# Value products over ranked experts, gathered by rank, with a register branch for each tile

## The chip, the cores and the metric

The kernel runs on one NeuronCore of one Trainium2 chip. The metric is the device time of one execution in microseconds, taken as the median over several runs of the same program. Profiles and traces are of one profiled execution each.

## The reference, cut to what matters

The program is two transformer blocks on 256 tokens of width 2048. Block 1 is a state-space mixer and a sparse attention; block 2 is a pair of linear-attention mixers followed by an expert layer (PEER) and a final normalisation. Only the expert layer is touched by the change:

```
xn: 256 tokens x 2048
s1, s2 = scores of 128 keys each, for 8 heads          # from xn @ w_query and the sub-keys
v1, i1 = top_k(s1, 16);  v2, i2 = top_k(s2, 16)
best, pos = top_k(v1[:, None] + v2[None, :], 16)        # 16 experts for each head and token
expert = i1[pos // 16] * 128 + i2[pos % 16]             # one of 16384
gate = softmax(best)
hid = gelu(xn . u_tab[expert])
y[token] = sum over heads and k of gate * hid * v_tab[expert]
out = rmsnorm(h + y) * g
```

A token uses 8 x 16 = 128 of the 16384 experts, so 128 tokens (one token tile) make 16384 choices, many of them of the same expert. `u_tab` and `v_tab` are 16384 x 2048 in float32, 128 MiB each.

## The kernel before

All large products are made from float32 operands in two float32r parts (high and low), three matmuls for one product. Weights come as blocks of [128, 1024] float32 (512 KB) through a `Stream` (class at line 43): SyncE loads a block into `raw` (line 138), ScalarE makes the high part `wh` (line 150), VectorE the low part `wl` (line 151); three buffers of each, refilled in the order of use. The stream's order is written down in `run` (line 1712): the weights of block 1, of block 2, then `pu` (the u table, 256 blocks) and `pv` (the v table, 256 blocks).

Instructions keep the order in which the program text issues them on each engine. Work that is to lie beside the matmuls is a Python generator in `self.bg`; `step()` (line 1031) issues its next piece, `behind()` (line 1036) the same but not ahead of the latest weight split and matmul. `mm_b` calls such a hook after each half tile of matmuls.

The expert layer (`peer`, line 1529) has these stages:

- Queries (`pqy`): 16 tiles, with the scores and the top-16 searches of the first token tile behind them.
- U stage (`u_phase`, line 1595): all 16384 experts, as 128 tiles of 128 experts, for all 256 tokens: `pu` [128 experts, 256 tokens] is 16 k-tiles x 3 = 48 matmuls of 128x128x256, then a gelu on ScalarE into `WA` (tiles 0 to 63) or `WB` (64 to 127) in SBUF. Behind the first 64 tiles lies the `routing` generator (line 1437: one piece a tile), which ends in `RT`: for each token its 128 slots' key numbers n1, n2 and the gate in three bfloat16 parts.
- Gates (`gates`, line 1495): for 4 tokens at a time VectorE builds one-hot matrices `gA` (key n2, line 1507) and `gB` (key n1, 64 values, times the three gate parts, lines 1508 and 1511); 12 matmuls of 64 columns (`pg`, line 1524) sum the gate of each expert, and VectorE multiplies them into `WA` (line 1526). For `WA` this lies behind the second half of the U stage, for `WB` behind the first half of the value stage.
- Value stage (lines 1619 to 1678): all 128 tiles of experts, in two halves x two column halves x 64 blocks. A block of V [128 experts, 1024 columns] is multiplied with the activations of its experts (`h`, split in two at lines 174 and 175): 2 token tiles x 2 column chunks x 3 = 12 matmuls of 128x128x512 into four PSUM accumulators (line 1655), so 24 for each tile of experts.
- The end (lines 1680 to 1697): the last three blocks are multiplied one token tile after the other, so that the first token tile is normalised and written while the second is still multiplied.

Every tile of experts is multiplied with both token tiles, whether or not a token is routed to one of its experts; the gate is then zero. The functions that the diff touches:

## Time and profile before

| what | value |
|---|---|
| median of three runs | 3203.23 us (3198.74 to 3209.94) |
| profiled execution, its own time | 3198.8 us |
| its span, first to last instruction | 3198.8 us |
| PE busy | 3098.4 us, 97% |
| DVE busy | 2201.7 us, 69% |
| ACT busy | 1447.2 us, 45% |
| POOL busy | 242.9 us, 8% |
| DMA | 531.90 MB, mean 166 GB/s |

PE is the TensorE matmul row, PEld its weight loads, DVE is VectorE, ACT ScalarE, POOL GpSimd, SP SyncE. Matmuls are pipelined, so the time of one in a row is longer than the pace at which they follow each other; the pace is read from their start times. A group of rows gives count, busy time and mean duration, then the idle time of the engine before them and who ended it.

### The profile page before, as it was taken

The page shows a single profiled execution, that of the slowest core. Times are in us where ns is not written, and L with a number is a line of the kernel's source. Part 1 is how long each engine was busy: PE and PEld are TensorE (multiplying, and loading weights), DVE is VectorE, ACT ScalarE, POOL GpSimd, SP SyncE. Part 2 cuts the span into 40 slices and gives each one's busy share as a digit, 9 for nine tenths or more (in the row PEclk, how much of TensorE's full clock was granted, in tenths as well). Part 3 has the DMA queues.
Part 4 walks back from the last instruction along what each step waited for, and adds up shares of the span by engine and source line. Part 5 has one row for each costly group of instructions (what it writes and reads, how often), then busy time and mean ns, then how long its engine had stood idle before and what let it go on. Part 6 is the DMA issues. An engine that isn't in the chain of part 4 may idle for free.

```text
span 3198.8 us, 52021 instructions
## 1 busy us (share of the span) xinstructions
PE 3098.4 (97%) x21016; PEld 2793.0 (87%) x21016; DVE 2201.7 (69%) x3382; ACT 1447.2 (45%) x2034; POOL 242.9 (8%) x171
## 2 busy tenths in 40 slices
PE   7988999999997999899999999999999999999998
PEld 7987899888786999788899999999998777788787
DVE  8857544555666763575586776588886999965655
ACT  4464333544445573354434444433334444444544
POOL 4453000000001000210001001000000000000000
PEclk8889999999998999999999999999999999999999
DMA  4134645434464543226655555555556555555554
GB/s 167 66 138 160 217 165 173 142 140 145 165 225 145 191 140 117 81 100 210 198 167 178 185 180 183 178 168 170 169 168 212 175 174 170 173 186 189 185 189 167
DMA packets 144465, 531.90 MB, mean 166 GB/s; under 512 B 16736, under 2 KB 17760, under 8 KB 141920
## 3 DMA queue, kind: packets, MB, share of 16 engines
q1 hardware_dynamic: 143648, 526.49, 49.2%
q8 instruction: 164, 2.69, 0.3%
q10 hardware_dynamic: 576, 2.10, 0.2%
q14 instruction: 77, 0.63, 0.1%
HBM read 522.23 MB, written 6.29 MB: 165 GB/s over the span
## 4 chain that ended last, share of the span: by engine, by line
PE 84%; issue 6%; DVE 6%; POOL 2%; ACT 2%; DMA 0%; POOLq 0%; DVEq 0%; ACTq 0%
PE pu L210 22%; PE acc L1655 22%; PE pz L225 9%; PE pq L210 4%; PE pso L225 4%; PE pqy L210 3%; PE pcv L210 3%; PE pk L210 2%; DVE wl L151 2%; PE pg L1524 1%; PE pi L225 1%; PE pv L225 1%; PE pf L210 1%; PE pz L1300 1%; PE pq L1289 1%
## 5 line engine op out<-in xcount | busy, mean ns | idle before, releaser
L151 DVE TENSOR_TENSOR wl<-raw,wh 128x1024 fp32r<-128x1024 f32 x940 | 1195.2, 1273 | 686.2 <-ACT wh L150 683.8
L150 ACT ACTIVATE wh<-raw 128x1024 fp32r<-128x1024 f32 x943 | 995.3, 1056 | 1130.3 <-PE pu L210 378.3
L210 PE MATMUL pu<-h,wh 128*128 128x256 f32 x4096 | 745.3, 283 | 1.3 <-ACT qy L1580 1.3
L1655 PE MATMUL acc<-wh,h 128*128 128x512 f32 x2040 | 659.2, 399 | 1.3 <-DVE h L175 0.7
L210 PEld LDWEIGHTS pu<-h,wh 128*128 128x128 f32 x4096 | 630.1, 188 | 1.5 <-ACT qy L1580 1.5
L210 PE MATMUL pu<-h,wl 128*128 128x256 f32 x2048 | 577.2, 282 | 1.4 <-DVE wl L151 1.4
L1655 PEld LDWEIGHTS acc<-wh,h 128*128 128x128 f32 x2040 | 384.4, 188 | 93.3 <-DVE h L175 1.1
L1655 PE MATMUL acc<-wl,h 128*128 128x512 f32 x1020 | 404.3, 396 | 0.0
L210 PEld LDWEIGHTS pu<-h,wl 128*128 128x128 f32 x2048 | 386.3, 189 | 2.2 <-DVE wl L151 2.2
L225 PE MATMUL pz<-wh,t 128*128 128x512 f32 x1024 | 335.9, 400 | 0.0
L1655 PEld LDWEIGHTS acc<-wl,h 128*128 128x128 f32 x1020 | 192.2, 188 | 43.9 <-DVE wl L151 0.3
L225 PEld LDWEIGHTS pz<-wh,t 128*128 128x128 f32 x1024 | 192.5, 188 | 40.6 <-issue 1.0
L225 PE MATMUL pz<-wl,t 128*128 128x512 f32 x512 | 201.4, 393 | 1.6 <-DVE wl L151 1.4
L225 PE MATMUL pso<-wh,t 128*128 128x512 f32 x640 | 200.6, 393 | 0.3 <-DVE th L984 0.3
L1511 DVE TENSOR_TENSOR gB<-gB,rt 128x256 bf16<-128x256 bf16 x384 | 151.1, 421 | 5.5
L174 ACT ACTIVATE h<-WA 128x256 fp32r<-128x256 f32 x127 | 52.8, 418 | 207.3 <-PE acc L1655 207.3
L225 PEld LDWEIGHTS pso<-wh,t 128*128 128x128 f32 x640 | 120.2, 188 | 27.1 <-DVE th L984 0.7
L210 PE MATMUL pq<-t,wh 128*128 128x256 f32 x768 | 138.1, 283 | 0.0
L174 ACT ACTIVATE h<-WB 128x256 fp32r<-128x256 f32 x128 | 53.6, 419 | 182.4 <-PE acc L1655 182.4
L225 PE MATMUL pso<-wl,t 128*128 128x512 f32 x320 | 124.8, 390 | 0.3 <-DVE wl L151 0.3
L210 PEld LDWEIGHTS pq<-t,wh 128*128 128x128 f32 x768 | 117.1, 188 | 0.7 <-issue 0.3
L225 PEld LDWEIGHTS pz<-wl,t 128*128 128x128 f32 x512 | 96.5, 188 | 22.6 <-DVE wl L151 2.3
(555 smaller groups left out, 4456.2 us busy)
## 6 DMA issues: line engine op xcount, KB each, us to landing
raw<-pu SPq DMA_DIRECT2D x256, 512.0 KB, 3.6
raw<-pv SPq DMA_DIRECT2D x256, 512.0 KB, 3.8
raw<-w_z SPq DMA_DIRECT2D x96, 512.0 KB, 3.2
raw<-w_fqi SPq DMA_DIRECT2D x48, 512.0 KB, 3.3
raw<-w_a_in SPq DMA_DIRECT2D x32, 512.0 KB, 3.3
raw<-w_q SPq DMA_DIRECT2D x32, 512.0 KB, 3.2
raw<-w_b_out SPq DMA_DIRECT2D x32, 512.0 KB, 4.0
raw<-w_conv SPq DMA_DIRECT2D x32, 512.0 KB, 3.2
```

The lines of the kernel that those rows point to most:

```text
L150: self.nc.scalar.activation(h, t, AF.Copy)
L151: m = (engine or self.nc.vector).tensor_tensor(l, t, h.bitcast(F32), op=OP.subtract).ins
L174: self.nc.scalar.activation(h, x, AF.Copy)
L210: mm = nc.tensor.matmul(ps, a[:, c], b(k), start=(k == 0 and n == 0), stop=(k == nk - 1 and n == len(ops) - 1))
L225: self.nc.tensor.matmul(pss[tt], x[a](k)[:, ts], b[:, kk * 512:(kk + 1) * 512], start=(k == 0 and n == 0), stop=(k == nk - 1 and n == 2))
L1289: pe.matmul(p4[:, g_], f8(N[c])[:, g_, :], half(Y8)[:, g_], start=True, stop=True)
L1300: pe.matmul(pz[:, g_, :], f8(Xs[c])[:, g_, :], Q8[:, g_, :], start=True, stop=True)
L1511: v.tensor_tensor(B[:, n], B[:, 0], bc(RT[2 + n][:, ts], 64), op=OP.mult)
L1524: pe.matmul(ps[:, j, :], A[:, j], B[:, n, j], start=(n == 0), stop=(n == 2))
L1655: pe.matmul(acc[t][e], x[:, t * 128:(t + 1) * 128], y[:, e * 512:(e + 1) * 512], start=(n == 0 and q == 0), stop=(n == 63 and q == len(ops ...
```

## The change

What it does, in the order of the program:

- `routing` is hooked twice for each U tile (as `behind` in `mm_b`) and so lies behind the first 32 tiles instead of 64. `RT` is one tile instead of five.
- The gelu of a U tile goes to a small buffer and from there by a DMA on ScalarE's queue to a DRAM tile `WG` [16384 experts, 512]: the first 256 columns of a row are the expert's activations for the 256 tokens.
- `gates` runs once, over all 128 values of n1, behind U tiles 32 and up, three pieces a tile. The one-hot matrices have the 4 tokens innermost. A further matmul a token (`cnt`) counts, for each expert and token tile, how often it is chosen. ScalarE copies the gates to a staging tile, and for each 64 tokens eight DMAs on ScalarE's queue write them to the second 256 columns of the rows of `WG`, in runs of 64 x 4 = 256 bytes. The product of gate and activation is no longer made here.
- `sort` (new) follows `gates`: it ranks the experts in four classes (chosen by both token tiles, by the first only, by the second only, by none), makes the list `idx` of expert numbers by rank, and four tile counts `cuts`, read into registers at U tile 123.
- The stream no longer holds `pv`. For each tile of 128 ranks GpSimd gathers the rows of V (8 KB each, [128, 2048]) and the rows of `WG` (2 KB each) by an indirect DMA; GpSimd multiplies gate and activation, ScalarE and VectorE split both operands.
- The value products of a tile lie in two `If` blocks on PE, one for each token tile (12 matmuls each: 4 column chunks x 3), the gathers and the split in `If` blocks of their engines. The ranks are taken in the order 0, 54, 1, 55, ..., 53, 107, 108, ..., 127. All eight accumulators [128, 512] are kept to the end, opened by eight matmuls of zeros.
- The end: both token tiles are added, normalised and written after the last product.

```diff
 # gates
+        nt, ng = 4, 64
...
+            A = P.tile([128, 128, nt], BF16, name="gA", bufs=2)
+            E = P.tile([128, 128, nt], BF16, name="gE", bufs=2)
+            B = P.tile([128, 3, 128, nt], BF16, name="gB", bufs=2)
+            bc = lambda n: RT[:, n, None, ts].to_broadcast([128, 128, nt])
+            v.tensor_tensor(A, self.iota4, bc(1), op=OP.is_equal)
+            v.tensor_tensor(E, self.iota4, bc(0), op=OP.is_equal)
+            v.tensor_tensor(B, E[:, None, :, :].to_broadcast([128, 3, 128, nt]),
+                            RT[:, 2:5, None, ts].to_broadcast([128, 3, 128, nt]), op=OP.mult)
...
+            A, E, B = AB.pop(b)
+            if b * nt % ng == 0:
+                st = self.stage.tile([128, 128, ng], F32, name="gst", bufs=2)
+            ps = self.psum.tile([128, nt, 128], F32, tag="g", name="pg", bufs=2)
...
+                    pe.matmul(ps[:, j, :], A[:, :, j], B[:, n, :, j], start=(n == 0), stop=(n == 2))
+                pe.matmul(cnt[:, half, :], A[:, :, j], E[:, :, j], start=(first and j == 0), stop=(last and j == nt - 1))
+            o = b * nt % ng
+            act.activation(st[:, :, o:o + nt], ps.rearrange("p t n -> p n t"), AF.Copy)
+            if o + nt == ng:
+                for n in range(0, 128, 16):
+                    t0 = b * nt + nt - ng
+                    nc.scalar.dma_start(G[n * 128:(n + 16) * 128, t0:t0 + ng].rearrange("(n p) t -> p n t", p=128),
+                                        st[:, n:n + 16, :])
 # sort (its core: 32 batches of 4 keys)
+            for o, a in ((A, 0), (E, 1)):
+                v.tensor_tensor(o, self.iota4, pb[:, a, None, ts].to_broadcast([128, 128, nt]), op=OP.is_equal)
+            v.tensor_tensor(B[:, 0:2], E[:, None, :, :].to_broadcast([128, 2, 128, nt]),
+                            self.nv[:, :, None, ts].to_broadcast([128, 2, 128, nt]), op=OP.mult)
...
+                pe.matmul(L, A[:, :, j], B[:, 0:2, :, j], start=(b + j == 0), stop=(b == nb - 1 and j == nt - 1))
 # peer
+        NR, NS, NV = 32, 78, 54
...
+        order = [j for n in range(NV) for j in (n, n + NV)] + list(range(2 * NV, 128))
...
+                raw[q] = vr.tile([128, D], F32, name="vraw", bufs=4)
+                with tc.If(reg["load"] > j):
+                    gp.indirect_dma_start(out=raw[q], out_offset=None, in_=i["pv"],
+                                          in_offset=bass.IndirectOffsetOnAxis(ap=idx[:, j:j + 1], axis=0))
...
+                wg[q] = vr.tile([128, 2, T], F32, name="wg", bufs=4)
+                with tc.If(reg["load"] > j):
+                    gp.indirect_dma_start(out=wg[q].rearrange("p a t -> p (a t)"), out_offset=None, in_=WG[:, :],
+                                          in_offset=bass.IndirectOffsetOnAxis(ap=idx[:, j:j + 1], axis=0))
...
+        for n in range(128):
+            ps = self.psum.tile([128, T], F32, tag="u", name="pu", bufs=2)
+            self.mm_b(ps, X, hook=(self.behind if n < NR else self.step) if n else None)
...
+            if n >= NR:
+                self.step()
+            w = rp.tile([128, T], F32, name="w", bufs=4)
+            act.activation(w, ps, AF.Gelu)
+            nc.scalar.dma_start(WG[n * 128:(n + 1) * 128, 0:T], w)
...
+                self.bg = chain(self.gates(rp, RT, WG[:, T:2 * T], cnt), self.sort(rp, cnt, idx, cuts))
+            elif n == 123:
+                self.finish()
+                regs()
+                for q in range(4):
+                    gather_v(q)
...
+            wh, wl = [vs.tile([128, D], F32R, name=n, bufs=3) for n in ("vwh", "vwl")]
...
+            with tc.If(reg["split"] > j):
+                gp.tensor_tensor(hm, g[:, 0], g[:, 1], op=OP.mult)
+                act.activation(hh, hm, AF.Copy)
+                v.tensor_tensor(hlo, hm, hh.bitcast(F32), op=OP.subtract)
+                act.activation(wh, r, AF.Copy)
+                v.tensor_tensor(wl, r, wh.bitcast(F32), op=OP.subtract)
...
+        def mm(q, t):
+            wh, wl, hh, hlo = hl[q]
+            ts = slice(t * 128, (t + 1) * 128)
+            for e in range(4):
+                es = slice(e * 512, (e + 1) * 512)
+                for a, b in ((hh, wh), (hh, wl), (hlo, wh)):
+                    pe.matmul(acc[t][e], a[:, ts], b[:, es], start=False, stop=True, skip_group_check=True)
+
+        prep(0)
+        for q in range(128):
+            j = order[q]
+            gather_v(q + 4)
+            gather_w(q + 3)
+            prep(q + 1)
+            with tc.If(reg["first"] > j):
+                mm(q, 0)
+            with tc.If(reg["end"] > j):
+                with tc.If((reg["both"] > j) | (reg["second"] <= j)):
+                    mm(q, 1)
...
+        for t in range(2):
+            for e in range(4):
...
+                v.tensor_tensor(o, o, acc[t][e], op=OP.add)
+                act.activation(acc[t][e], o, AF.Square, accum_out=sq[:, t, e:e + 1])
```

## Rows read from the trace of the kernel before

**Rows 1.** The page: busy time of each engine, and granted TensorE clock by slice.
```profile
PE 3098.4 (97%) x21016; PEld 2793.0 (87%) x21016; DVE 2201.7 (69%) x3382; ACT 1447.2 (45%) x2034; POOL 242.9 (8%) x171
PEclk8889999999998999999999999999999999999999
```

**Rows 2.** Busy time by stretch: U stage (four stretches), value stage (two), end, queries.
```profile
core 0: us, PE busy (x) PEld busy (x) DVE busy (x) ACT busy (x) POOL busy (x), PEclk, DMA share, GB/s
1670.70:1738.00 67.30, 66.99 (x559) 66.79 (x558) 45.51 (x66) 27.71 (x35) 5.22 (x2) 1.00 0.55 174
1738.00:2051.00 313.00, 311.91 (x2596) 311.28 (x2595) 206.34 (x346) 134.98 (x168) 18.84 (x11) 1.00 0.58 182
2051.50:2402.00 350.50, 350.50 (x3460) 347.42 (x3459) 306.21 (x491) 134.53 (x169) 0.00 (x0) 1.00 0.54 169
2439.00:2790.00 351.00, 349.78 (x2131) 273.90 (x2130) 337.29 (x606) 156.57 (x231) 0.00 (x0) 1.00 0.53 181
2790.00:3190.00 400.00, 399.88 (x1715) 320.69 (x1711) 241.33 (x294) 196.12 (x292) 6.86 (x5) 1.00 0.55 182
1580.00:1670.00 90.00, 88.83 (x745) 88.63 (x743) 74.17 (x205) 34.72 (x45) 4.22 (x7) 1.00 0.57 179
```

**Rows 3.** PE in order of time, at the seam of U and value stage (start, us).
```profile
2438.72 0.29 PE L210 MATMUL pu<-h,wl 128*128 128x256 f32 x1
2438.84 0.40 PE L210 MATMUL pu<-h,wh 128*128 128x256 f32 x2
2439.08 0.28 PE L210 MATMUL pu<-h,wl 128*128 128x256 f32 x1
2439.20 3.60 PE L1655 MATMUL acc<-raw,WA 128*128 128x512 f32 x8
2442.63 0.86 PE L1524 MATMUL pg<-gB,gA 128*128 128x64 bf16 x24
```

**Rows 4.** Groups of instructions by line, U stage with routing (1672 to 2050).
```profile
L151 DVE TENSOR_TENSOR wl<-raw,wh 128x1024 fp32r<-128x1024 f32 x130 | 175.9, 1358 | 122.4 <-ACT wh L150 120.9
```

**Rows 5.** The same, U stage with gates (2051.5 to 2402).
```profile
L151 DVE TENSOR_TENSOR wl<-raw,wh 128x1024 fp32r<-128x1024 f32 x112 | 136.4, 1218 | 0.0
L150 ACT ACTIVATE wh<-raw 128x1024 fp32r<-128x1024 f32 x113 | 119.8, 1060 | 217.5 <-PE pu L210 164.2 <-DVE gB L1508 51.3 <-DVE wl L151 2.0
L1511 DVE TENSOR_TENSOR gB<-gB,rt 128x256 bf16<-128x256 bf16 x189 | 74.6, 422 | 4.1
L1507 DVE TENSOR_TENSOR gA<-iota,rt 128x512 bf16<-128x512 bf16 x63 | 43.0, 682 | 0.0
```

**Rows 6.** The same, second half of the value stage (2800 to 3180).
```profile
L175 DVE TENSOR_TENSOR h<-WB,h 128x256 fp32r<-128x256 f32 x128 | 56.1, 438 | 78.5 <-ACT h L174 78.5
L174 ACT ACTIVATE h<-WB 128x256 fp32r<-128x256 f32 x128 | 53.6, 419 | 182.4 <-PE acc L1655 182.4
```

**Rows 7.** Single lines: count, duration in ns min/median/max, first and last start.
```profile
L1605 ACT ACTIVATE WB<-pu x64: 363/366/370, 2049.6 to 2441.1; 128x256 f32<-128x256 f32 x64
L1432 POOL TENSOR_TENSOR cand<-val x16: 619/624/627, 1595.0 to 1909.6; 128x256 f32<-128x256 f32 x16
L138 SPq DMA_DIRECT2D raw<-pv x256: 327/328/885, 2427.2 to 3175.7; - x128
```

**Rows 8.** ScalarE's DMA issues in order of time: start, us, count.
```profile
0.73 2.33 ACTq L297 DMA_DIRECT2D t<-xT  x4
```

**Rows 9.** DMA queues (packets, MB, share of 16 engines) and issues (KB, us to landing).
```profile
q8 instruction: 164, 2.69, 0.3%
raw<-pv SPq DMA_DIRECT2D x256, 512.0 KB, 3.8
ident<-ident SPq DMA_DIRECT2D x2, 64.0 KB, 3.7
```

**Rows 10.** The end in order of time: start, us, instruction.
```profile
3189.68 1.28 DVE L1645 TENSOR_TENSOR h<-h,acc 128x512 f32<-128x512 f32 x2
3189.77 0.39 PE L1655 MATMUL acc<-wh,h 128*128 128x512 f32 x1
3192.77 1.28 DVE L1687 SCALAR_TENSOR_TENSOR h<-h,ssf,h 128x1024 f32<-128x1024 f32 x1 [0.67 <-POOL ssf L604]
3194.32 0.43 SPq L1688 DMA_DIRECT2D out<-h  x1
```

**Rows 11.** A stretch in which PE waits, columns as in the stretches above.
```profile
960.00:1040.00 80.00, 62.33 (x394) 54.76 (x393) 55.72 (x86) 43.18 (x69) 15.03 (x13) 0.89 0.41 144
```

More of the change, by code (lines that the diff above doesn't have):

```diff
@@ L17 @@
 AX = mybir.AxisListType
+ET = mybir.EngineType
 PSUM = bass.MemoryType.PSUM
@@ L1608, in peer @@
[L1608 to L1619 removed]
+        rt = lambda shape, name, dt=F32: rp.tile([128] + shape, dt, name=name)
@@ new lines, in peer, with regs @@
+        gp.memset(self.ones, 1.0)
+        gp.memset(self.smask, 1.0)
+        gp.memset(self.smask[:, :, 0:1], 0.0)
+        mhalf = rt([2], "mhalf2")
+        gp.memset(mhalf, -0.5)
+        RT = self.RT = rt([5, T], "rt", BF16)
+        idx = rt([128], "idx", U32)
+        cuts = rt([4], "cuts", I32)
+        WG = self.dram.tile([16384, 2 * T], F32, name="WG")
+        left, stage = ExitStack(), ExitStack()
+        NR, NS, NV = 32, 78, 54
+        reg = {}
+        def regs():
+            for k, n, engines in (("both", 0, (ET.PE,)), ("first", 1, (ET.PE,)), ("second", 2, (ET.PE,)),
+                                  ("end", 3, (ET.PE,)), ("load", 3, (ET.Pool,)),
+                                  ("split", 3, (ET.Activation, ET.DVE, ET.Pool))):
+                reg[k] = nc.values_load(cuts[0:1, n:n + 1], engines=engines, min_val=0, max_val=128)
@@ L1625, in peer @@
         sq = self.small.tile([128, 2, 4], F32, name="sqf")
-        order = [(half, c, n) for half in range(2) for c in range(2) for n in range(64)]
-        parts = {}
-        def part(m):
-            if m < len(order):
-                half, c, n = order[m]
-                if m == 0:
-                    parts[m] = W[half][:, n, :]
-                    return
-                r = ring[:, m % 4]
-                self.split(r[:, 0], r[:, 1], W[half][:, n, :])
-                parts[m] = r
-        self.bg = self.gates(rp, W[1], RT, 64)
@@ L1658, in peer @@
-        te = [(t, e) for t in range(2) for e in range(2)]
-        late = []
-        for m, (half, c, n) in enumerate(order):
-            if n == 0:
-                acc = [[self.psum.tile([128, 512], F32, tag="acc", name="acc", bufs=4) for _ in range(2)] for _ in range(2)]
-            if m + 2 == 128:
-                self.finish()
-            part(m + 2)
-            w, r = s.get(), parts.pop(m)
-            if m + 3 >= len(order):
-                late.append((n, w, r))
-                continue
-            for t, e in te:
-                mm(n, w, r, t, e)
-            if not half:
-                self.step(1 + (n % 8 == 0))
-            if n == 63:
-                for t, e in te:
-                    done(half, c, t, e)
@@ L1678, in peer @@
-        ss = self.small.tile([128, 2], F32, name="ssf")
-        def write(t):
+        stage.close()
+        vs = right.enter_context(tc.tile_pool(name="vs", bufs=1, side="right"))
+        pes.close()
+        self.psum = pes.enter_context(tc.tile_pool(name="psum3", bufs=1, space=PSUM))
+        acc = [[self.psum.tile([128, 512], F32, name=f"acc{t}{e}") for e in range(4)] for t in range(2)]
+        z = vs.tile([128, 512], BF16, name="zero")
+        gp.memset(z, 0.0)
+        for q in range(3):
+            gather_w(q)
@@ L1681, in write @@
+        ss = self.small.tile([128, 2], F32, name="ssf")
+        for t in range(2):
+            for e in range(4):
+                cs = slice(e * 512, (e + 1) * 512)
+                o = hs[t][:, cs]
+                v.tensor_tensor(o, o, acc[t][e], op=OP.add)
+                act.activation(acc[t][e], o, AF.Square, accum_out=sq[:, t, e:e + 1])
+                if e < 2:
+                    gp.tensor_tensor(o, o, fg[:, cs], op=OP.mult)
             r = ss[:, t:t + 1]
@@ L1727, in run @@
             s.add(i[n])
-        pv = i["pv"].rearrange("(n p) d -> n p d", p=128)
-        for half in range(2):
-            for c in range(2):
-                pvc = pv[64 * half:64 * half + 64, :, c * 1024:(c + 1) * 1024]
-                if half + c == 0:
-                    s.add(pvc[0:1], split=False)
-                    pvc = pvc[1:]
-                s.add(pvc)
         g1 = ExitStack()
```

187 lines of the change are left out of this document (116 added, 71 removed).

## The prediction

> **What bounds the kernel now.** I read the page first: PE is busy 97% of the span and its granted clock is full from the first third on [rows 1]. Then the stretches [rows 2]: in the U stage and in the value stage PE is busy for all but some 2 us in 1430, while DVE ranges from 60 to 96% and the DMA engines from 53 to 58%. So in both stages the number of matmuls times their pace is the time, and no wait has to be looked for. The paces are start-to-start times: 0.12 us for a 128x128x256 product of the U stage [rows 3], 400/1715 = 0.233 us for a 128x128x512 product [rows 2], 0.86/24 = 0.036 us for a gate product of 64 columns [rows 3]. The U stage runs from 1670.7 to 2439.2 us [rows 2, 3], 768.5 us; its 128 x 48 products make 737 of them, 768 gate products 28. The value stage runs to 3190.2 (last product, [rows 10]), 751 us, and 8.6 us of normalising and writing follow to 3198.8.
>
> **How many products are left.** This is a count of the data, not a time. I followed the reference's routing on its given inputs: 6376 experts are chosen by both token tiles, 3694 by the first only, 3757 by the second only, 2557 by none. The class borders lie at 6376, 10070 and 13827, so the tile counts are 50, 79 (first), 78 (start of the second) and 109. The first token tile needs 79 tiles, the second 50 + 31 = 81: 160 of 256 half tiles, 1920 products instead of 3072. Nineteen tiles of 128 are empty.
>
> **Value stage.** 1920 x 0.233 = 448 us on PE instead of 751: **-303**. What comes next behind PE, for each of 109 tiles, against PE's 448/109 = 4.1 us:
> - DMA: 1 MB of V and 0.25 MB of WG, 1.31 million bytes. A stretch with 182 GB/s at a share of 0.55 gives 331 GB/s for a full share [rows 2], so 4.0 us. This is the next limit, 4% away.
> - DVE: a low part of twice the size, 2 x 1.22, and one activation split 0.44 [rows 5, 6]: 2.9 us. ACT: 2 x 1.06 + 0.42 = 2.5 us [rows 5, 6].
> - GpSimd: 0.62 for the product [rows 7] and the issue of two gathers. No DMA issue by GpSimd is in the trace. From below, SP holds 0.33 us for one [rows 7]; ScalarE 2.33/4 = 0.58 [rows 8]; from above, an issue that holds GpSimd until it lands costs 3.8 [rows 9]. I take 0.58, the nearest issue row: 1.8 us a tile; the range is 1.3 to 8.2.
> - Branches: no row shows one. PE has 12 products, 2.8 us, ahead of a jump if the operands are there, so I take the 58 jumps over one arm in the 109 tiles as hidden; from above a jump waits for code as for a DMA, up to 3.7 us [rows 9].
>
> The order pairs 24-product tiles with 12-product tiles and four buffers of V smooth the rest, but with DMA at 96% of PE's time I add 5%: **+22**.
>
> **U stage.** Gates: 768 products of now 128 columns and 256 counts, 1024 in all. Their price lies between 0.036 (if the weight load sets the pace) and 0.072 (if the columns do); half the 256-column pace is 0.06, and I take it: 61 us. The sort adds 128 products of 256 columns at 0.12: 15 us. Of the 28 us of gates that stood here nothing remains, and 4 us of scores and seams stay: 737 + 61 + 15 + 4 = 817 against 768.5, **+49** (from +24 to +61). What lies beside these products:
> - Routing now has 32 tiles x 5.76 = 184 us. DVE needs 64 x 1.36 = 87 for low parts [rows 4]; its other work in the first 380 us was 45.5 + 206.3 - 175.9 = 76 [rows 2, 4], some 4 of it gates. That is 159 of 184 us, 86%. The queries had the same density of pieces: DVE 74.2 of 90 us, PE 88.8 [rows 2]. 1.3% of 184: **+3**.
> - Gates: a tile now has 1.5 batches of 16 products, 5.76 + 1.44 = 7.2 us on PE. DVE: 512 elements in 0.68 and 256 in 0.42 [rows 5], so 1536 in 1.72 at the same slope; 2 x 1.22 + 1.5 x (0.68 + 0.68 + 1.72) = 7.1 us. It is near the limit even if the new layout brings nothing; before, DVE ran at 337 of 351 us with PE losing 1.2 [rows 2]. **+3**.
> - ScalarE: 2 x 1.06, the gelu 0.37 [rows 7], the new PSUM copy of 512 columns at most twice that, 0.73 x 1.5, one DMA issue for WG 0.58 and 8 in 10.7 tiles for the gates 0.43: 4.6 of 7.2 us. Hidden, as long as an issue costs what [rows 8] show. The gates' DMAs have 2048 runs of 256 bytes where those had 128, and their 65536 runs share the DMA engines with the U table: **+10**, from 0 to the price of the third rival.
>
> **The seam.** Before, the first value product followed the last U product at once [rows 3]. Now the last gelu ends 2.4 us after the last product starts [rows 3, 7], its way to WG takes 0.58 + 3.7 (issue [rows 8], a 64 KB landing [rows 9]), the first gather 0.58 + 3.8, the product and the split 0.62 + 0.42 + 0.44: 12.5 us. If PE must wait for the whole block, another 2.1 + 2.4 for the V parts, 17. I take **+13**, and for the granted clock **+3**: in a stretch where PE idled 17.7 of 80 us the clock was 0.89, a loss of 0.11 x 62 = 7 [rows 11].
>
> **The end.** Before, the last product (3189.8) had two adds beside it, 0.64 each [rows 10]. Now eight adds follow it, and the first token tile's normalising no longer lies beside products. 6 x 0.64 = 3.8 and half of one chain of 3189.7 to 3194.3 [rows 10]: **+6** (0 to 10). The 19 empty tiles at the end of the order cost five branches each on PE and the engines that feed it: **+8** (0 to 70, at 3.7 each).
>
> **Sum**, against the profiled execution: 3198.8 - 303 + 22 + 49 + 3 + 3 + 10 + 13 + 3 + 6 + 8 = 3009.8. The median before is 4.4 above that execution, so 3014 for a median.
>
> **Rivals.**
> 1. *GpSimd paces the value stage.* For it: POOL is nearly idle before (8%), so its price for a gather is untested, and it stands in one queue with the product that PE waits for. At 2.2 us a gather, the middle of the bounds, a tile takes 5.0 us, 547 instead of 470: 3091. Against it: the other queues' issues are far shorter [rows 7, 8]. It turns slower beyond (470 + 189)/109 = 6.0 us a tile, 2.7 us a gather; at 3.8 it is 3438.
> 2. *Jumps cost PE a code fetch.* The trace shows 164 instruction packets of 16 KB that took 0.3% of 16 engines' 3198.8 us, 0.94 us each [rows 9]. With 58 + 38 jumps over an arm, each at 0.94 with nothing hidden: +90 - 8, 3096. At 3.7, a landing: 355 - 8, 3361. It decides for slower from 2.0 us a jump. Against it: an arm is only 24 instructions with their weight loads, and the target lies just behind it. The Trainium skill (Runtime: NRT & Kernel Launch, Instruction fetch mechanics) says that prefetch is sequential and that a taken branch whose target is not in the current window of pages waits for a DMA. No row here has a branch, so the trace neither bears it out nor denies it.
> 3. *The gates' writes hold ScalarE's queue; the other side.* An issue of 128 runs holds it 0.58 us [rows 8]; if the time goes with the runs, one of 2048 holds it 9.3, eight in a row 74. The weight splits stand behind them; three buffers cover two blocks, 7.2 us. PE then waits 67 us four times: 268 instead of 10, 3272, slower. It decides from 7 us an issue. For it: nothing in the trace has so many runs. Against it: descriptors may be made after the issue, off the queue. The Trainium skill (DMA: Bandwidth & Descriptors, Specifications) gives 512 bytes as the least for line rate, with a read-modify-write below; the runs here have 256. No row shows a write that small.
> 4. *Everything hides.* Gates at 0.036 and no losses but the seam: 3198.8 - 303 + 24 + 12.5 = 2932.
>
> **Chances.** Forecast 0.55 (2950 to 3060), rival 1 0.2 (a quarter of it slower), rival 2 0.1 (half slower), rival 3 0.07, rival 4 0.08. A difference under 0.3%, 10 us, can't be told from none. Faster 0.55 + 0.15 + 0.05 + 0.08 = 0.83, slower 0.05 + 0.05 + 0.07 = 0.17, of which I give 0.02 to no change. The range 2935 to 3180 holds the forecast, most of rival 4 and the faster parts of 1 and 2.
>
> **What would show it.** In the changed profile: 1920 products of 512 columns, with starts 0.233 us apart inside an arm; a value stage of about 470 us; a gap on PE of 13 us ahead of it; DMA at 0.9 or more of its share there. If PE's idle time in the value stage is put down to the POOL product or to a gather, rival 1 holds; if to nothing ("issue") at the starts of arms, rival 2; if PE idles for some 60 us four times between U tiles 42 and 75, with ACT's queue in DMA issues, rival 3. A value stage over 660 us makes the prediction wrong in sign, a U stage over 850 us in its second term.

## The result and the profile after

| | before | forecast | after |
|---|---|---|---|
| median, us | 3204.6 (4 runs) | 3014 | 3227.3 (4 runs, 3226.8 to 3233.9) |
| profiled execution, its span | 3198.8 | | 3225.7 (own time 3227.6) |
| U stage (first U product to last) | 768.5 | 833 | 937.5 (1669.0 to 2606.5) |
| seam | 0 | 16 | 14.5 (to 2621.1) |
| value stage (first product's start to last's) | 751 | 470 | 503.8 (to 3124.8) |
| from there to the end | 9 | 23 | 100.9 |

The changed kernel is slower: 1.0075 times before, 95% interval 1.0059 to 1.0091. The forecast column adds up my terms by stretch. The 303 us of value products did go, but the three other stretches took them back: 104 us more than forecast in the U stage, 34 in the value stage, 78 behind the last product.

The page after, beside [rows 1]: 1525 products fewer on PE, which is still busy 91% of a longer span.

```profile
PE 2944.7 (91%) x19491; PEld 2668.9 (83%) x19496; DVE 1895.3 (59%) x2632; ACT 1376.7 (43%) x1806; POOL 677.7 (21%) x502
PEclk9889999999998999999999999999899999999985
```

The stretches after, columns as in [rows 2]: U with routing, U with gates, U with the sort and after it, value stage, end.

```profile
1669.00:1861.00 192.00, 188.06 (x1535) 186.00 (x1536) 165.97 (x337) 81.97 (x101) 26.76 (x13) 0.99 0.62 194
1861.00:2300.00 439.00, 411.76 (x3314) 397.98 (x3313) 243.39 (x356) 147.40 (x204) 0.53 (x1) 0.94 0.58 164
2300.00:2606.00 306.00, 304.75 (x2467) 296.95 (x2466) 140.33 (x146) 117.23 (x148) 5.13 (x4) 1.00 0.65 202
2640.00:3100.00 460.00, 424.06 (x1795) 329.73 (x1794) 266.39 (x201) 222.35 (x200) 397.72 (x301) 1.00 0.80 287
3125.00:3225.70 100.70, 0.46 (x2) 0.00 (x0) 8.78 (x14) 7.33 (x18) 6.96 (x6) 0.52 0.06 22
```

Three rows want an explanation: PE idles 27 of 439 us beside the gates, where it idled for next to nothing; it idles 36 of 460 us beside the value products, while GpSimd is the engine with the next highest load (398); and at the end no engine works for 86 of the 100 us.

**U stage, the products.** In `pe.matmul(out, a, b)`, `a` is the stationary operand (its load is a PEld row) and `b` the moving one. PE in order of time (the number behind x is a count), then the gates' lines:

```profile
1929.21 0.30 PE L1530 MATMUL cnt<-gE,gA 128*128 128x128 bf16 x1
1929.33 0.53 PE L1529 MATMUL pg<-gB,gA 128*128 128x128 bf16 x3
1929.68 0.29 PE L1530 MATMUL cnt<-gE,gA 128*128 128x128 bf16 x1
```
```profile
L1529 PE MATMUL pg<-gB,gA 128*128 128x128 bf16 x768 | 122.8, 297 | 11.9 <-ACT gst L1532 11.9
L1512 DVE TENSOR_TENSOR gB<-gE,rt 128x1536 bf16<-128x1536 bf16 x62 | 59.4, 958 | 1.8
L1615 PE MATMUL pL<-gB,gA 128*128 128x256 bf16 x56 | 14.2, 405 | 8.9 <-DVE gB L1602 4.5 <-DVE gE L1601 4.3
```

From one count product to the next are four products and 0.47 us: 0.118 us each, where I took 0.06. A batch of 16 so costs 1.89 us; the starts of the gelus say the same, 7.65 us apart for a tile with one batch and 9.55 with two, over 5.76 for a bare tile, one with its 48 products alone. The sort's 256-column products are 0.228 apart (0.12 taken). VectorE's build, which I had feared at 1.72 us [rows 5], takes 0.96.

**U stage, the writes.** ScalarE in order of time at the first full group of 64 tokens, and the stretch around it:

```profile
1957.27 17.64 ACTq L1536 DMA_DIRECT2D WG<-gst  x8
1975.02 1.06 ACT L152 ACTIVATE wh<-raw 128x1024 fp32r<-128x1024 f32 x1 [17.78 <-DMA WG<-gst]
```
```profile
1950.00:1990.00 40.00, 34.13 (x266) 33.12 (x264) 17.15 (x23) 11.70 (x16) 0.00 (x0) 0.87 0.79 203
```

Eight issues hold ScalarE's queue for 17.6 us, 2.2 each against 0.58 in [rows 8]; the weight split stands behind them, PE runs dry, and the granted clock of the stretch is 0.87. This happens four times, and each time the granted clock is 0.5 for a while after PE has run dry (10, 10, 10 and 24 us), which is the lower of its two levels, 1.2 of 2.4 GHz.

**Value stage.** For each tile `hm` is the product of activation and gate, `hh` and `hlo` its high and low part, `vwh` and `vwl` those of V. PE's waits (total, times, longest), then the lines beside it:

```profile
PE acc L1799 <- PEq L1807: 18.8, 26, 1.4
PE acc L1799 <- PEq L1810: 12.7, 22, 0.7
PE acc L1799 <- ACT hh L1787: 2.9, 3, 1.6
PE acc L1799 <- ACT vwh L1789: 1.3, 1, 1.3
```
```profile
L1790 DVE TENSOR_TENSOR vwl<-vraw,vwh 128x2048 fp32r<-128x2048 f32 x101 | 231.1, 2289 | 88.8 <-ACT vwh L1789 88.8
L1729 POOL DMA_INDIRECT wg<-WG,idx x100 | 166.8, 1668 | 23.1 <-issue 15.2 <-POOL hm L1786 5.7 <-PE acc L1799 1.9
L1721 POOL DMA_INDIRECT vraw<-pv,idx x101 | 161.1, 1595 | 38.6 <-issue 30.0 <-DVE hlo L1788 4.1 <-PEq L1807 2.5
L1786 POOL TENSOR_TENSOR hm<-wg 128x256 f32<-128x256 f32 x100 | 71.9, 747 | 0.9
```

PEq is PE's sequencer, L1807 and L1810 are the two branches of a tile. Of PE's waits 31.5 us carry its name, 4.2 that of ScalarE's splits, and none that of a DMA. The sequencer passed 552 compare-and-branch instructions, 515 of them in the value stage and 37 behind it, 0.14 us each on average.

**The end** in order of time; in [rows 10] the last write was issued 5 us after the last product:

```profile
3124.82 0.63 PE L1799 MATMUL acc<-vwh,hlo 128*128 128x512 f32 x1
3141.82 3.68 DVE L1818 TENSOR_TENSOR h<-h,acc 128x512 f32<-128x512 f32 x6 [20.50 <-PEq L1807]
3208.70 0.56 POOL L606 TENSOR_TENSOR ssf<-rs_a,mhalf 128x1 f32<-128x1 f32 x1 [88.30 <-POOLq L1785]
```

The sums start 17 us late, when PE has passed its empty arms. But the norm's power, a column of 128 numbers on GpSimd, waits 62 us more with its operand ready at 3146.2. GpSimd's own queue holds it: for each gather that is not made, the other arm of the branch raises the semaphore that the DMA would have raised. The sequencer's records show 38 of these, 3103.1 to 3207.6:

```
start us, us
3103.10 2.42 POOL sequencer L1728 INC_SWDGE_SEM
3105.73 2.38 POOL sequencer L1720 INC_SWDGE_SEM
...
3205.20 2.39 POOL sequencer L1720 INC_SWDGE_SEM
```

### The profile page after: what moved, and what is told of

The parts are those of the page before. It is cut to its first block, busy times and chain, and to the rows that moved or that the text cites. A ratio compares the mean times of both kernels' runs of the same rounds, so it can differ in the third digit from the quotient of the medians.

```text
span 3225.7 us, 51109 instructions
## 1 busy us (share of the span) xinstructions
PE 2944.7 (91%) x19491; PEld 2668.9 (83%) x19496; DVE 1895.3 (59%) x2632; ACT 1376.7 (43%) x1806; POOL 677.7 (21%) x502
## 5 line engine op out<-in xcount | busy, mean ns | idle before, releaser
L153 DVE TENSOR_TENSOR wl<-raw,wh 128x1024 fp32r<-128x1024 f32 x685 | 885.8, 1296 | 790.3 <-ACT wh L152 785.7
L152 ACT ACTIVATE wh<-raw 128x1024 fp32r<-128x1024 f32 x688 | 728.7, 1060 | 1156.0 <-PE pu L212 385.0
L1790 DVE TENSOR_TENSOR vwl<-vraw,vwh 128x2048 fp32r<-128x2048 f32 x109 | 249.6, 2290 | 103.6 <-ACT vwh L1789 103.6
L1799 PE MATMUL acc<-vwh,hh 128*128 128x512 f32 x640 | 257.9, 403 | 57.1 <-PEq L1807 18.8
L1799 PE MATMUL acc<-vwh,hlo 128*128 128x512 f32 x640 | 252.8, 395 | 0.0
L1799 PE MATMUL acc<-vwl,hh 128*128 128x512 f32 x640 | 251.3, 393 | 0.0
L1729 POOL DMA_INDIRECT wg<-WG,idx x109 | 178.8, 1640 | 259.0 <-DMA WG<-w 233.6
L1789 ACT ACTIVATE vwh<-vraw 128x2048 fp32r<-128x2048 f32 x109 | 208.3, 1911 | 18.4 <-PE acc L1799 11.7
L1721 POOL DMA_INDIRECT vraw<-pv,idx x109 | 171.3, 1571 | 136.7 <-PE pu L212 96.0
L1799 PEld LDWEIGHTS acc<-vwl,hh 128*128 128x128 f32 x640 | 121.2, 189 | 23.0
```

The costliest lines, as they stand in the source:

```text
L152: self.nc.scalar.activation(h, t, AF.Copy)
L153: m = (engine or self.nc.vector).tensor_tensor(l, t, h.bitcast(F32), op=OP.subtract).ins
L1721: gp.indirect_dma_start(out=raw[q], out_offset=None, in_=i["pv"], in_offset=bass.IndirectOffsetOnAxis(ap=idx[:, j:j + 1], axis=0))
L1729: gp.indirect_dma_start(out=wg[q].rearrange("p a t -> p (a t)"), out_offset=None, in_=WG[:, :], in_offset=bass.IndirectOffsetOnAxis(ap=idx ...
L1789: act.activation(wh, r, AF.Copy)
L1790: v.tensor_tensor(wl, r, wh.bitcast(F32), op=OP.subtract)
```

## The experiments

All start from the changed kernel unless said. The times of before in the five sets are 3200.1 to 3203.9 us, so differences to 3227 carry some 4 us of doubt; the ratios are to before.

**1. The loop ends at the last tile in use** (`e1_tail`; fits this data alone).
```diff
-        order = [... for n in range(NV) ...] + list(range(2 * NV, 128))
+        order = [... for n in range(NV) ...] + [2 * NV]
```


> The value loop ends at rank tile 108, the last one that this data takes; the 19 tiles that no half takes are left out of the loop, so their branches aren't there. Nothing else differs. Theory (GpSimd's untaken gathers make the end): after the changed kernel's last product, GpSimd passes 38 untaken gather arms at 2.38 to 2.42 us, some 90 us, before it starts the final norm; so the stretch from the last product to the end of the span falls from 101 us to 13 to 25, and the time to 3135 to 3155 us. Rival a (TensorE's empty arms make it): the sums of the residual start 17 us after the last product, since TensorE passes the same arms; if these are what counts, the time falls by 15 to 20 us, to about 3210. Rival b (something behind the norm makes it): the norm's own chain is late for another reason, and the time stays within 5 us of 3227.

3146.3 us, 0.9831 [0.9815, 0.9847]. From the last product to the end 18.2 us instead of 100.9. Theory right: 81 us, and PE's 17 us of empty arms are the small part of it. (An arm is what one branch guards; it is empty when the branch leaves it out.)

**2. One branch round the last 16 tiles** (`e7_outer_branch`; holds for any data).
```diff
+        run(0, 112)
+        with tc.If(reg["all"] > 112):
+            ... gathers, splits and products of tiles 112 to 127
```


> The last 16 of the 128 rank tiles, with their gathers, splits and products, stand in one branch per engine on whether any tile beyond 112 is needed; the other 112 tiles, 3 of them empty, keep a branch each. So 6 untaken gathers are left singly and 32 go with one branch. Theory (each untaken gather costs GpSimd its 2.4 us because its semaphore is raised one by one): if the outer branch raises each semaphore once, the tail falls from 101 us to 15 to 35, 3145 to 3165; if its other arm raises the semaphore once for each gather left out, 32 times 2.4 us stay and the time is 3205 to 3225. With the loop that ends at tile 108 (3146 us) as the lower end.

3159.6 us, 0.9873 [0.9856, 0.9889]; end 28.2 us, as the theory had it. The sequencer shows the six single raises and then one, 2.40 us, for all of the 32 gathers left out. So the price goes by the branch, not by the gather. PE's sequencer takes 3.8 us, once, for the jump over this long arm.

**3. Moving operands laid out by token** (`e2_mov_contig`), **and the mirror** (`e3_wts_contig`). In the first, E, B and the sort's B are `[128, token, 128]`, A stays `[128, 128, token]`; in the second A alone is laid out by token.
```diff
-                    pe.matmul(ps[:, j, :], A[:, :, j], B[:, n, :, j], ...)
+                    pe.matmul(ps[:, j, :], A[:, :, j], B[:, n, j, :], ...)   # first
+                    pe.matmul(ps[:, j, :], A[:, j, :], B[:, n, :, j], ...)   # second
```


> The moving operands of the one-hot products (E, its three products with the gates, and those of the sort) are laid out with the 128 columns of a token side by side; the stationary operand A keeps its step of four elements, and the number and shape of the products are unchanged. Theory (the moving operand's step of 8 bytes sets the price): the gate and count products fall from 0.118 us apart to about 0.06, 1024 of them give back 55 to 65 us, the sort's from 0.228 to about 0.12, 128 of them 10 to 15; the time falls by 55 to 75 us, to 3150 to 3175. Against it stands that VectorE now builds E and B with operands repeated along the last axis, which may cost it up to twice 1.38 us a step. Rival a (the load of the stationary operand sets the price, one for each product): nothing falls, 3220 to 3235. Rival b (VectorE's builds pace the steps): the stretch grows.

> The mirror of the run with contiguous moving operands: only the stationary operand A of the gate and count products is laid out with the 128 columns of a token side by side; the moving operands keep their step of four elements. Theory (the moving operand's step sets the price): the products stay 0.118 us apart and the time within 10 us of 3227. Rival a (the load of the stationary operand sets it): they fall to about 0.06 and the time to 3160 to 3175.

First 3182.1 us, 0.994 [0.9923, 0.9956]; second 3222.9, 1.0068 [1.0051, 1.0084]. A tile with one batch takes 6.73 us in the first, so a batch 0.97 and a product 0.061; in the second 7.61, a product 0.115. The moving operand's step sets the price. The first gained 45 us, not 55 to 75: its writes still stall PE four times, and VectorE's builds grew (B 1.76 us, E 0.68 a batch). How much each of the two takes back was not measured apart.

**4. The operands change places** (`e12_swap`): A moving and by token, B and E stationary with their step; the sums, the writes and the rank logic transposed.
```diff
+                    pe.matmul(ps[:, j, :], B[:, n, :, j], A[:, j, :], ...)
```


> The two operands of the one-hot products change places: the second index's one-hot (A) is moving and laid out with a token's 128 columns side by side; B and E are stationary and keep their step of four, so VectorE's big build stays as it was (0.96 us a step; it took 1.76 with B laid out by token). The sums come out transposed, and the writes, the ranks and the index follow that. Theory (only the moving operand's step sets the price of a product): the products are 0.06 us apart as with contiguous B and E, and VectorE is freed of 0.8 us a step: 3227 less 45 to 65, 3162 to 3182, at or below the 3182 of contiguous B and E. Rival (three stationary operands with a step for one moving operand cost as much): 3215 or more.

3175.0 us, 0.9912 [0.9893, 0.9931]. As expected: 16 products from 0.06 apart, and VectorE's big build back at 0.96 us.
```profile
1930.94 0.22 PE L1532 MATMUL cnt<-gA,gE 128*128 128x128 bf16 x1
1931.00 0.33 PE L1531 MATMUL pg<-gA,gB 128*128 128x128 bf16 x3
1931.17 0.22 PE L1532 MATMUL cnt<-gA,gE 128*128 128x128 bf16 x1
```

**5. The gates' writes, four ways.** `e4_spread_writes`: one a step on ScalarE's queue; `e6_sp_writes`: in a row on SyncE's; `e10_sync_spread`: half as large, one a step, on SyncE's; `e11_gp_writes`: in a row on GpSimd's.
```diff
-                    nc.scalar.dma_start(G[n * 128:(n + 16) * 128, ...], st[:, n:n + 16, :])
+                    nc.gpsimd.dma_start(G[n * 128:(n + 16) * 128, ...], st[:, n:n + 16, :])   # e11
```


> The eight writes of the gates that follow each 64 tokens are issued one a step (two a tile) instead of eight in a row; same bytes, same runs, same queue (ScalarE's). Theory (the row of eight holds ScalarE's queue for 15 to 18 us, and with it the split of X that TensorE needs): an issue of 2.0 to 3.2 us a step fits beside ScalarE's other work, the four gaps of 12 to 15 us between the products of tiles 42 to 76 go, and with them the stretches at half clock: 45 to 55 us, 3172 to 3182. Rival (the transfers themselves, 2048 runs each, are too slow, whenever they are issued): each step waits for ScalarE instead, the 32 issues keep their 75 us in all, and the time stays within 15 us of 3227.

> The 32 writes of the gates are issued on SyncE's queue instead of ScalarE's, eight in a row as in the changed kernel; nothing else differs. Theory as it stands after the spread writes gained 9 us only (each issue holds the engine that makes it for 2 to 3 us, in a row or apart, and ScalarE has no such time to spare beside the splits of X): the four gaps between the products of tiles 42 to 76 go, and their stretches at half clock, since SyncE issues only the loads of raw tiles, 5.8 us apart: from 924 us for the first to the last gelu to 880 to 890, the time 3180 to 3195. Rival a (a row of eight on SyncE holds the raw tiles back by 16 to 20 us instead): the gaps stay, within 10 us of 3227. Rival b (the writes' 65,536 runs of 256 bytes load the DMA engines, and the raw tiles land late): gaps too, but VectorE and ScalarE wait for DMA in them.

> The writes of the gates on SyncE's queue, each group of 64 tokens in 16 pieces of eight rows (1024 runs of 256 bytes), one piece a step, so that a group's 4.2 MB go out while the next group is made. Theory (the row of writes fills the DMA engines faster than they empty, later issues on any queue then stand, and raw tiles come late: with ScalarE one a step the gaps shrank from 51 us beyond the products' price to 34, on SyncE in a row to 22): spread over 16 steps, some 90 us, nothing stands, the excess falls to under 8 us, and the time to 3178 to 3190. Rival (a queue that issues writes of short runs holds up its own other transfers however thin they are spread): 3195 to 3215.

> The same writes, eight in a row as in the changed kernel, issued by GpSimd, which has nothing else to do in that stage; neither ScalarE's nor SyncE's queue holds one. Theory (what costs is the DMA engines' time on 65,536 runs of 256 bytes in bursts): the raw tiles still come late in the bursts, and half or more of the 51 us of excess stays: 3195 to 3215, unless GpSimd's making of the descriptors spreads them by itself. Rival (what costs is the queue of the engine that issues): all of it goes, 3172 to 3182.

| | us | ratio [95%] | U tiles 32 to 95 over a bare 5.76 each |
|---|---|---|---|
| changed kernel | 3227.3 | 1.0075 | 190 us |
| e4, ScalarE, spread | 3218.4 | 1.0056 [1.0039, 1.0072] | 175 |
| e6, SyncE, in a row | 3201.9 | 0.9997 [0.9987, 1.0006] | 160 |
| e10, SyncE, spread | 3191.7 | 0.9963 [0.9951, 0.9976] | 156 |
| e11, GpSimd, in a row | 3190.4 | 0.9962 [0.9949, 0.9976] | 157 |

The products' own price is 64 x 1.89 + 32 x 0.91 = 150 us, so the writes cost the changed kernel 34 (against e11) to 40 us, the stretches at half the clock included; the 51, 34 and 22 us in the expectations are another count of the same excess. By their times e4's rival held, e6 and e11 lie between the ranges of theory and rival, and e10 is 2 us above its theory's. My first theory (the row of eight) did not come true in e4: there ScalarE waits for raw tiles. Its waits in e4, e6 and e11:
```profile
ACT wh L152 <- DMA raw<-pu: 40.9, 13, 8.3
```
```profile
ACT wh L152 <- DMA raw<-pu: 16.8, 5, 12.8
```
```profile
ACT wh L152 <- DMA raw<-pu: 7.6, 3, 3.8
```
e6 has its gap too, four tiles of 25 to 27 us, because the raw tiles' issues now stand behind the writes on one queue. e4 was hardly thinner than the row, either: a group's packets start over 20 to 24 us, against 19 in the changed kernel and 39 to 51 in e10. e10 and e11 lose nearly all of the cost. The first burst of the changed kernel, then that of e11:
```profile
1957.00:1985.00 28.00, 22.13 (x164) 21.29 (x163) 11.40 (x18) 6.26 (x10) 0.00 (x0) 0.82 0.95 235
```
```profile
1959.00:1987.00 28.00, 28.00 (x236) 27.60 (x236) 15.10 (x20) 10.65 (x14) 9.46 (x8) 1.00 0.98 288
```
The DMA engines are as full in e11 (0.98 against 0.95), and PE loses nothing. So my theory was wrong: their load alone isn't what costs. Whether it is the queue, as my rival said, is not shown, for the packets changed with it. The changed kernel, then e11:
```profile
DMA packets 216662, 574.38 MB, mean 178 GB/s; under 512 B 84240, under 2 KB 101776, under 8 KB 200144
```
```profile
DMA packets 155226, 574.41 MB, mean 180 GB/s; under 512 B 18704, under 2 KB 36240, under 8 KB 138704
```
65,536 packets of 256 bytes are gone: a group's 16,384 are recorded as 1024 of 4096 bytes, though the runs in DRAM are the same. No run separates queue and packets; e10 shows that packets of 256 bytes on SyncE's queue cost little when they are spread. GpSimd's issues take 1.15 us each, and its landing is later, 14.0 us against 6.4, which costs nothing there. What the extra issue time on ScalarE's queue consists of no run tells.

**6. PE's branches and GpSimd's product.** `e5_static_pe` writes this data's counts into PE's program; `e8_hm_dve` makes hm on VectorE; `e9_static_hm` does both.
```diff
-            with tc.If(reg["first"] > j):          # e5, e9
+            if j < 79:
-                gp.tensor_tensor(hm, g[:, 0], g[:, 1], op=OP.mult)   # e8, e9
+                v.tensor_tensor(hm, g[:, 0], g[:, 1], op=OP.mult)
```


> TensorE's branches of the value loop are replaced by the counts that this data gives (both 50, first 79, second from 78, end 109), written into the program; the branches of GpSimd, ScalarE and VectorE stay, and the same 1920 products run. Theory (TensorE's branch arithmetic is some 31 us of the value stage, and GpSimd stands close behind it): the 31.5 us of waits for TensorE's own sequencer go, the products come 448 to 460 us from first to last unless GpSimd takes over, which needs 9.2 us for a pair of tiles against 8.4 of TensorE; the last one decides the gain: 10 to 31 us, 3196 to 3217. The tail keeps its 90 us of untaken gathers and loses little. Rival (GpSimd paces the stage and TensorE's branches lie in its shadow): the waits move to the split of the activations and the gathers, under 8 us gained, 3220 or more.

> The product of hidden activations and gates (hm, 109 times 749 ns on GpSimd) is made by VectorE; gathers and all else stay. Theory (GpSimd's 9.2 us for a pair of tiles lies over TensorE's 8.4, so GpSimd shares in the pace of the value stage): without hm GpSimd needs 7.7 us a pair, VectorE's addition is below 0.5 us a tile and it has 15 per cent to spare; the stage loses 5 to 25 us of its 504, and the end loses a few as the last hm no longer stands behind untaken gathers: 3195 to 3220. Rival (TensorE's own branches pace it): under 5 us, 3222 to 3230.

> Both edits of the two runs before: TensorE's branches of the value loop written in as counts, and hm on VectorE. Alone, the first cost 80 us (3307) and the second gave 10 (3217). Theory (with TensorE's branches gone, each hm on GpSimd ran together with VectorE's vwl and took 2.69 us instead of 0.75, and the chain hm, hh, vwh, vwl closed into a loop of 5.4 us a tile; so it was the meeting of the two engines, not the missing branches, that cost): without hm on GpSimd the loop is open, the products are TensorE's 448 us and little more, 450 to 470 from first to last instead of 495 to 504, and the time 3170 to 3195. Rival (static products cost TensorE itself more, or GpSimd's gathers, which also grow beside vwl, 0.95 to 2.3 us, pace the stage): 3215 or more.

e5 3307.0 us, 1.033 [1.0313, 1.0347]; e8 3217.5, 1.0052 [1.0035, 1.0069]; e9 3168.2, 0.9897 [0.988, 0.9913]. The value stage takes 580, 495 and 445 us. e8 came out as expected; e9 came 2 us under its range, with a stage 5 us shorter than expected. e5 went against both theory and rival: less work and 80 us slower. Its lines of hm and of PE's wait, and a tile in order of time:
```profile
L1786 POOL TENSOR_TENSOR hm<-wg 128x256 f32<-128x256 f32 x86 | 231.1, 2687 | 1.8
L1799 PE MATMUL acc<-vwh,hh 128*128 128x512 f32 x517 | 215.6, 417 | 73.2 <-ACT hh L1787 73.2
```
```profile
2800.10 2.44 DVE L1790 TENSOR_TENSOR vwl<-vraw,vwh 128x2048 fp32r<-128x2048 f32 x1 [1.45 <-ACT vwh L1789]
2800.28 2.85 POOL L1786 TENSOR_TENSOR hm<-wg 128x256 f32<-128x256 f32 x1
2803.16 0.42 ACT L1787 ACTIVATE hh<-hm 128x256 fp32r<-128x256 f32 x1 [3.10 <-POOL hm L1786]
2803.53 1.92 ACT L1789 ACTIVATE vwh<-vraw 128x2048 fp32r<-128x2048 f32 x1
2805.48 2.46 DVE L1790 TENSOR_TENSOR vwl<-vraw,vwh 128x2048 fp32r<-128x2048 f32 x1 [1.45 <-ACT vwh L1789]
```
hm starts beside vwl and ends only when vwl has ended, 2.85 us instead of 0.75 (2.69 on average). hh waits for it, vwh stands behind hh on ScalarE, the next vwl behind that, and the next hm again meets it: a ring of 5.4 us a tile, 109 times 588. In the changed kernel, which differs in PE's branches alone, only 2 of the 109 hm fall beside a vwl. GpSimd's gathers grow in the same way, 0.95 to 1.0 us alone and 2.1 (V) or 2.4 (WG) beside vwl, medians of the changed kernel. The Trainium skill (SBUF — State Buffer, SBUF: two separate sides) says that VectorE and GpSimd share a port pair, locked for a whole instruction, among others where VectorE has two operands in SBUF and GpSimd reads there too; e5 agrees (2.69 against 0.75 us), and e9, where only hm's engine differs, shows what it costs: 139 us.

**7. The four edits together, branches as they are** (`e13_all_fixes`: 2, 4, e11, e8), **and with fewer or none.** `e14_fewer_branches` and `e15_two_tests` put the ranks in another order, so that PE needs one comparison a half tile; e14 also drops the other engines' branches, e15 keeps them, always taken. `e16_all_static` has this data's counts on PE.
```diff
-                with tc.If(reg["end"] > j):                    # e14, e15
-                    with tc.If((reg["both"] > j) | (reg["second"] <= j)):
-                        mm(q, 1)
+                with tc.If(reg["second"] <= j):
+                    mm(q, 1)
```


> The changed kernel with its branches as they are, and four edits that each ran alone: operands of the one-hot products swapped (alone 3175), the gates' writes on GpSimd (3190), the last 16 tiles in one outer branch (3160), hm on VectorE (3217). Theory (each of the terms is a stretch of its own and they add): 3227 less 52, 37, 68 and 10 is 3060, so 3045 to 3075; the value stage stays 490 to 505 us, since TensorE's branches are untouched. Rival (one takes back what another gives: VectorE with hm and the larger build, or GpSimd's writes beside it, becomes late): above 3085.

> As the run with all four edits, and the ranks put in the order first half only, both, second half only, so that a tile needs one comparison for each half; the branches on whether a tile is needed at all (gathers, splits, TensorE) go: the three empty tiles of the first 112 are gathered and multiplied with gates of zero. TensorE passes two branches a tile instead of three with a compound test, and makes 36 products more (3 half tiles, 8.4 us). Theory (the value stage's 504 us over TensorE's 448 are its branches, at 0.07 to 0.43 us a comparison, 425 of them; the run with none of them and hm on VectorE took 445): half of the branches gone gives 20 to 28 us, the three tiles take 8: 10 to 20 us below the run with all four edits. Rival (it was hm alone on GpSimd, or the place of the pair in the loop, and the number of branches doesn't count): within 4 us of it or slower by the 8 us.

> As the run with all four edits, but the ranks in the order first half only, both, second half only, and on TensorE one comparison a half tile (two a tile instead of three, none compound). Unlike the run with fewer branches, GpSimd, ScalarE and VectorE keep a branch at every place, one that is always taken, so that their order of work stays; the three empty tiles are multiplied with gates of zero, which adds 8.4 us of products. That run lost 43 us with 45.5 us of waits for hlo, which VectorE then made after vwl of the tile before. Theory (the loss was that order, and TensorE's comparisons do cost): no wait for hlo; a comparison of the three and the compound test gone, 15 to 25 us, less 8: 3025 to 3040, against 3044. Rival (the loss was the three empty tiles or the new order of ranks): 3060 or more.

> As the run with all four edits, and TensorE's branches written in as this data's counts (both 50, first 79, second from 78, end 109); the other engines keep theirs. Nothing else differs from that run, so the difference is the price of TensorE's branches with hm on VectorE. Theory (they are what lies between the stage's 493 us and TensorE's 448): the stage takes 445 to 452 us, 2990 to 3005 in all. Rival (without hm on GpSimd the branches hide): within 10 us of 3044.

| | us | ratio [95%] | value stage |
|---|---|---|---|
| e13 | 3044.3 | 0.9505 [0.9489, 0.9521] | 493 us |
| e14 | 3087.4 | 0.964 [0.9622, 0.9658] | 543 |
| e15 | 3062.4 | 0.9567 [0.9543, 0.9591] | 518 |
| e16 | 2991.2 | 0.9345 [0.9321, 0.9369] | 445 |

e13 beats both kernels, holds for any data, and is 16 us below what the parts add up to (3060). These lie in the U stage: with the operands swapped the writes on ScalarE's queue cost more (U tiles 32 to 95 take 132 us over bare ones in e12, 84 in e13) than without (190 and 157). e16, which came out as expected, differs from e13 in PE's branches alone: they cost 48 us. By starts of products, the first product of an arm comes later than the pace inside an arm by 45 us in all in e13, and by nothing in e16. PE's waits in e13, e16, e14 and e15 (value stage):
```profile
PE acc L1806 <- PEq L1814: 21.3, 28, 1.4
PE acc L1806 <- PEq L1817: 13.7, 24, 0.7
```
```profile
PE acc L1806 <- DVE vwl L1797: 3.8, 7, 1.0
```
```profile
PE acc L1803 <- DVE hlo L1792: 40.1, 44, 1.0
```
```profile
PE acc L1807 <- DVE vwl L1798: 23.8, 31, 1.0
PE acc L1807 <- PEq L1815: 11.2, 31, 0.7
PE acc L1807 <- PEq L1817: 7.7, 24, 0.4
```
Both forecasts for fewer comparisons were wrong in total; in e15 the rival's time came true. There the waits for the sequencer fell from 35 to 19 us, as the theory said, but 24 us of waits for vwl took their place, and three tiles more are multiplied (8 us). From 2600 to 2760 PE makes 289 products in 80 us, where e13 makes 320 and 324; from 2840 to 3000 it makes 331, where e13 makes 317 and 303. So the loss lies in the part in which tiles that only the first half takes alternate with full ones, and the gain behind it. In that part ScalarE's vwh waits 4.6 us until PE has released a buffer, and PE then stands before the vwl made from it. That points to the order of the ranks, but order, tests and the three tiles changed in one run, so it isn't shown. e14 has waits for hlo on top; why its splits come so late without the branches is not settled.

## Why the prediction was wrong

By its own steps:

- **Value products, -303: right.** 1920 products; without branches and with hm elsewhere they take 445 us (e9, e16), against my 448. That they agree so closely is partly luck: inside an arm the pace is 0.227 us and not 0.233, so the products take 436, and some 10 us of gaps make up for it.
- **Value stage, +22 for DMA: wrong in cause and size.** The DMA share is 0.80, not 0.9 or more. What costs is what I set at nothing, "the 58 jumps over one arm in the 109 tiles as hidden", behind 2.8 us of products: PE's branches, 48 us (e13 against e16). The step missed that every test costs, 515 in the stage, and that a branch at the end of a tile isn't hidden by products that stand before it: the next tile's products wait for the sequencer. GpSimd's part is 9 us (e8): a gather takes it 1.6 us on average, between my 0.58 and the 2.2 of rival 1. Rival 2's place was right (the arms), but its mechanism wasn't seen in the changed kernel: 0.14 us a comparison, no landing of 3.7 us; the longest wait is 1.4. Only the jump over 16 tiles in e7, e13, e14 and e15 takes as long, 3.3 to 3.8 us, once a run.
- **Gates and sort, +49: mis-sized.** "half the 256-column pace is 0.06, and I take it" holds for a moving operand whose columns lie side by side (0.061 in e2), not for one with a step of four bf16 elements (0.118). The layout with the token innermost, which makes VectorE's build cheap, doubles PE's price; I weighed it for VectorE only. 150 us instead of 76: 74 of the 104 us that the U stage went over.
- **The gates' writes, +10: mis-sized.** 34 to 40 us. I took the price of an issue with 128 runs for one with 2048. Rival 3 had the right place (four gaps, ScalarE's queue) and too high a price, 9.3 us an issue; it is 2.2. The rule of the Trainium skill that I set beside it (DMA: Bandwidth & Descriptors, Specifications: 512 bytes as the least for line rate) isn't what decides here: the same runs of 256 bytes leave the U tiles 6 us over the products' price when they are spread on SyncE's queue (e10), and 7 us from GpSimd's (e11).
- **Routing, +3:** 192 us for 32 tiles, +8.
- **Seam, +13 and +3: right**, 14.5 us, with PE waiting for the first hh. GpSimd's gather had waited 233 us for the writes of WG, which delayed nothing else.
- **The end, +6 and +8: the step that failed most.** I priced the 19 empty tiles as branches "on PE and the engines that feed it", and asked nothing about what an arm that is not taken still has to do. On GpSimd it raises the DMA's semaphore, 38 x 2.39 = 91 us, 82 of them behind the last product, and GpSimd holds the norm. 78 us over; experiments 1 and 2 take it away.

Together 74 + 26 (writes) + 5 (routing) + 34 + 78 is 217, less some 3 for the seam and an earlier start of the U stage. What they have to account for is 213 us, for my sum was wrong as well: its terms add up to 3012.8, not 3009.8, and 3012.8 to 3225.7 is 213; the forecast should have read 3017. (PE's idle time that I read from [rows 2] is 2.7 us in 1482, not 2 in 1430. Neither slip matters.) Either of the terms of 74 and 78 us alone decided the sign: e12, where the products come at the pace that I took, stands at 3175 us, and e1, without the untaken gathers, at 3146, both faster than before. With all four edits it stands at 3044, against my 3014.

## What to carry to other kernels

Price both arms of a branch on every engine: the arm that skips a DMA still has work, and one branch round many costs as one. Ask of a layout what each reader pays, the matmul's moving side above all, and let the operand that no engine wants strided be the stationary one. When an edit that only removes work makes a kernel slower, look for two engines whose instructions now meet.

## What the runs showed of the hardware that I had not expected

- A bf16 product of 128 columns is 0.118 us from the next with a moving step of four elements, 0.061 without; a stationary operand with that step costs next to nothing (0.118 against 0.115).
- An untaken gather costs GpSimd 2.39 us, a gather made 0.95 to 1.0 alone and 2.1 to 2.4 beside vwl: left out, it is no cheaper. One branch round 32 gathers costs 2.40 in all.
- A DMA issue of 2048 runs takes 2.2 us on ScalarE's queue and 1.15 on GpSimd's, where the same bytes are recorded in packets of 4096 bytes instead of 256.
- A GpSimd product of 0.75 us takes 2.85 when it starts beside a VectorE subtraction with two operands in SBUF, which takes 2.3 us alone and 2.4 there.
- A compare-and-branch of PE's sequencer takes 0.14 us on average (0.07 to 0.43); one that leaves out the arms of 16 tiles takes 3.3 to 3.8.
